# The first mixer's order without memory units, and the memory's products in the later mixer

## The chip, the cores and the metric

The kernel runs on one NeuronCore of a Trainium2 chip. The metric is the device time of one execution in microseconds; all times here are microseconds unless marked ns. Of the core's engines, TensorE (PE) does matrix products and transposes, with its weight loads (PEld) overlapping; VectorE (DVE) and ScalarE (ACT) do elementwise work and evictions; GpSimd (POOL) does little; SyncE (SP) issues nearly all transfers. Each engine runs its instructions in the order in which they were put on it, and waits at the first whose inputs or buffers are not ready.

## The reference

Two blocks in a row over one sequence of 256 tokens of width 1024, all in fp32. The first has two layers; a layer is a mixer, a residual with layer norm, a feed-forward (a dense SwiGLU in layer 0, eight experts with the top two per token in layer 1), and another residual with layer norm:

```
proj = x @ w_in        # columns for three branches
o_a  = gated delta rule (6 heads, 4 chunks of 64 tokens; S_c+1 depends on S_c), normed, times silu(gate)
u    = glu_a * sigmoid(glu_b);  u = causal depthwise conv of 31 taps + bias;  o_b = silu(layer_norm(u))
o_c  = softmax attention (6 heads, causal, decayed by a cumulative log-sigmoid)
mix  = (concat(o_a, o_b, o_c) * mix_scale) @ w_out
```

The second block has two layers too. Its mixer computes, besides a local attention, an attention over a memory: `k, v = split(rms_norm(mem) @ w_mem_kv)`, with four heads of 128 columns for k and 512 columns for v. The memory is an input, so k and v of both layers can be computed at any time before they are used.

## The kernel before

All weights are streamed once from HBM, in the order in which they are used, by transfers on SP's queue into four buffers called `raw`. A product is done in one of two ways. A split product first takes the weights apart, `hi` on ACT (L202) and `lo` on DVE (L206), and then does three matmuls in a reduced fp32 form (`mm3`: high with high, high with low, low with high). A whole product takes `raw` as it is, in one fp32 matmul instruction that the profile lists as two records; in the first mixer these read `x,raw`, and in a memory unit `raw` alone. The matmul line is L217 for all of them, so one goes by the names of tiles.

The first mixer (`_mixer1`, for l = 0 and 1) begins with the split projections for q, k and v of the gated delta rule. Then it prepares that rule's chunks: powers of a triangular matrix for its inverse (`XT`, `A`, `X`, `zc`), decays (`dec`), and the transformed keys and values. Then come the chunk steps: `ps_sm<-vn,kd` (c0, and then c1 and c2), each followed on DVE by `S<-S,eg,ps_sm`, then on PE by `S,wT` and on DVE by `vn<-u,ps_sm`. In between, work that doesn't depend on it is put in by a table: `fill(p)` (called from `gdn` and once behind it with `REST`) reads a string letter by letter. A letter c takes the next piece of the remaining projections, each of them 4 whole or 8 split products: first for the attention's values, then the rest of the delta rule's v, the attention's q and k in three groups, the convolution's two inputs (`gb`, `ga`, from which DVE makes `uu`), and the gate. An x takes the next step of the attention's six heads: scores and mask on PE, `fmx` on DVE, exponential `fp` on ACT, a reciprocal and a scaling on DVE, three transposes on PE, and for each pair of heads the product with the values (`fpT,fv`). A digit n takes n steps of the convolution: first `cvacc<-uu,cdwh,pc`, then 30 taps, each of two DVE instructions. U loads the memory (`mem_load`, with a scaling on ACT), and u does one memory unit (`mem_units`): a quarter of the memory's k and v of one layer, 16 whole products of 256 columns, evicted on ACT (`kvt`) and sent from ACT's queue to a buffer `kv` in HBM. The table `UNITS` says which units are done where: b3 to b5 lie in the blocks behind, m0 and m1 in the first mixer of layers 0 and 1.

After `REST` come the statistics of the convolution (`ps_st<-cst,cvacc`), its layer norm, the gated output of the delta rule (`og`), and the product with `w_out`.

Which instruction stands where on an engine is set when the program is built: a scheduler takes, for each engine, ready work in the order of the program, from a model of durations. So a change in the table moves the instructions of all engines near it.

In the second block's mixer, `mem_kv` makes k and v of the memory: for the units that were done it loads `kv` (L1652) and scales it into `km` and `vm`; for those that were not, it loads the memory (L1660), splits it (`mmh` on ACT, `mml` on DVE) and does split products.

Of the kernel before, what the change touches and what calls it, by code (L numbers as in the profile page):

```python
# [160 lines left out]
FREE = 1  # L161
PRE = 2
FILL = ({'s': 'cccc', 'g': 'cccccc'}, {'s': 'cccc', 'g': 'cccccc'})
REST = 'ccccxccxcxcxcxcxcxcxcccx33x33U333c3c3c3cu999u'
WHOLE = ('wwwpppwwpw', 'pwwpppwwpw')
PG = 2
MO = 6
# [1 line left out]
XRG = 6  # L169
SPLIT = 4  # L170
SPARE = ('xgh', 'xgl')
UNITS = {'b1': (), 'b2': (), 'b3': ((0, 0), (0, 1)), 'b4': ((0, 2),), 'b5': ((0, 3),), 'm0': ((1, 0), (1, 1)), 'm1': ((1, 2), (1, 3))}
SETUP = (2, 5)

SHIFT = 8
# [5 lines left out]
class K:  # L181
# [478 lines left out]
    def ffn_block1(self, l):  # L660
        with self.phase() as self.ph:
            z, st, ev = self.resid_ln()
            self.ffn('s1', 'ffn_w1', 'ffn_w3', 'ffn_w2', l, ev, mid=self.mem_stats,
                     mid2=(lambda: self.mem_load('b2')) if UNITS['b2'] else None)
            b = self.ln_finish(st, D, 1e-5)
# [61 lines left out]
    def _mixer1(self, l, first):  # L727
# [90 lines left out]

        units = list(UNITS[f"m{l}"])
        box = {}  # L820

        def fill(p):
            for n in p:
                if n == 'c':
                    next(stream, None)
                elif n == 'x':
                    next(box['fox'], None)
                elif n == 'U':
                    self.mem_load(f"m{l}")
                elif n == 'u':  # L830
                    if units:
                        self.mem_units(f"m{l}", [units.pop(0)])
                else:
                    for _ in range(int(n)):
                        next(conv, None)
# [34 lines left out]
        oS = self.gdn(l, qkv, lr, g, lnb, fill)  # L870
        fill(REST)
        mh, ml = self.new_hl()
# [727 lines left out]
    def mem_load(self, *at):  # L1600

        self.mts = {}
        for l in sorted(set(l for a in at for l, _ in UNITS[a])):
            mt = self.raw().rearrange("p (k t) -> p k t", k=KD)
# [5 lines left out]
    def mem_units(self, at, us=None):  # L1610


        for l, u in us or UNITS[at]:
            mt = self.mts[l]
# [372 lines left out]
```

## Time and profile before

| what | us |
|---|---|
| median of three runs | 2951.46 (2949.2 to 2954.4) |
| profiled execution | 2954.75, its span 2952.9 |
| PE busy | 2894.1 (98%), 19525 instructions |
| PE's weight loads busy | 2628.7 (89%) |
| DVE busy | 2155.8 (73%) |
| ACT busy | 1754.5 (59%) |
| mean granted clock of PE | 0.983 |

Busy is the time in which an engine has work; matmuls overlap, so that their listed durations add to more than the time from one start to the next. What an instruction costs in a dense stretch is read from the starts of its neighbours. The granted clock is the share of full speed (2.4 GHz) that the chip allowed PE; 0.50 is its lower level, 1.2 GHz.

### The profile page before, as it was taken

What the parts mean: (1) busy time and instruction counts of PE and PEld (TensorE: products, weight loads), DVE (VectorE), ACT (ScalarE), POOL (GpSimd) and SP (SyncE); (2) the same over time, 40 slices, a digit from 0 to 9 for tenths busy, and PEclk for the clock granted to TensorE, in tenths of its full rate; (3) what the DMA queues carried; (4) which work ended last, traced back from release to release, by engine and by line L of the source; (5) the groups of instructions that cost most, each with busy time, mean ns of one, the idle gap of its engine ahead of it and who ended that gap; (6) DMA issues with size and microseconds to landing.
All of it is one profiled execution on the core that took longest, in us unless ns stands there. A gap on an engine that the chain in (4) does not pass through costs nothing.

```text
span 2952.9 us, 48784 instructions
## 1 busy us (share of the span) xinstructions
PE 2894.1 (98%) x19525; PEld 2628.7 (89%) x19525; DVE 2155.8 (73%) x3156; ACT 1754.5 (59%) x2582; POOL 79.8 (3%) x142
## 2 busy tenths in 40 slices
PE   8999999999999999999999999999999999999998
PEld 7889998887888887788878899989999999999998
DVE  6476566479989888988889866676766665867764
ACT  5335445258787777778777744565554444655543
POOL 1100002000000000000000000100000000100000
PEclk9899999899999999999999999999999999999999
DMA  6035542158989997998999755534655555335553
GB/s 226 22 136 186 188 151 99 38 225 350 345 339 358 362 359 296 361 353 331 357 368 357 275 175 188 177 108 158 211 188 192 184 191 193 137 110 194 203 189 112
DMA packets 104205, 663.77 MB, mean 225 GB/s; under 512 B 11808, under 2 KB 17952, under 8 KB 28576
## 3 DMA queue, kind: packets, MB, share of 16 engines
q1 hardware_dynamic: 101664, 658.46, 60.6%
q8 instruction: 156, 2.56, 0.3%
q10 hardware_dynamic: 2304, 2.10, 0.2%
q14 instruction: 81, 0.66, 0.1%
HBM read 657.36 MB, written 3.15 MB: 224 GB/s over the span
## 4 chain that ended last, share of the span: by engine, by line
PE 57%; DVE 2%; ACT 1%; issue 0%; POOL 0%; POOLq 0%; DVEq 0%; ACTq 0%
PE ps_mm L217 47%; PE py L217 5%; PE ps_fx L217 2%; PE ps_sm L217 2%; DVE lo L206 1%; PE ps_fx L227 0%; PE ps_sm L227 0%; DVE aa L1784 0%; ACT hi L202 0%; DVE gi L206 0%; PE ps_st L217 0%; DVE aa L206 0%; ACT xr L203 0%; DVE y L214 0%; DVE ffab L206 0%
## 5 line engine op out<-in xcount | busy, mean ns | idle before, releaser
L206 DVE TENSOR_TENSOR lo<-raw,hi 128x1024 fp32r<-128x1024 f32 (+2 forms) x1216 | 1434.3, 1207 | 384.2 <-ACT hi L202 371.8
L202 ACT ACTIVATE hi<-raw 128x1024 fp32r<-128x1024 f32 (+2 forms) x1216 | 1246.8, 1044 | 622.0 <-PE ps_mm L217 466.7
L217 PE MATMUL ps_mm<-xh,hi 128*128 128x256 f32 x2736 | 777.1, 285 | 13.1 <-ACT hi L202 8.1
L217 PE MATMUL ps_mm<-xh,lo 128*128 128x256 f32 x2736 | 770.2, 282 | 2.1 <-DVE lo L206 2.1
L217 PE MATMUL ps_mm<-xl,hi 128*128 128x256 f32 x2736 | 771.8, 282 | 0.3 <-DVE xl L206 0.3
L217 PEld LDWEIGHTS ps_mm<-xh,hi 128*128 128x128 f32 x2736 | 519.5, 190 | 19.7 <-ACT hi L202 8.8
L217 PEld LDWEIGHTS ps_mm<-xh,lo 128*128 128x128 f32 x2736 | 518.6, 190 | 5.7 <-issue 2.7
L217 PEld LDWEIGHTS ps_mm<-xl,hi 128*128 128x128 f32 x2736 | 520.5, 190 | 3.5 <-issue 2.0
L217 PE MATMUL ps_mm<-lo,xgh 128*128 128x512 f32 x896 | 356.5, 398 | 0.7
L217 PE MATMUL ps_mm<-hi,xgl 128*128 128x512 f32 x896 | 349.8, 391 | 0.0
L217 PE MATMUL ps_mm<-hi,xgh 128*128 128x512 f32 x896 | 349.6, 392 | 0.0
L217 PE MATMUL ps_mm<-ffl,hi 128*128 128x256 f32 x880 | 245.6, 279 | 0.0
L217 PE MATMUL ps_mm<-ffh,hi 128*128 128x256 f32 x880 | 245.6, 279 | 0.0
L217 PE MATMUL ps_mm<-ffh,lo 128*128 128x256 f32 x880 | 245.5, 279 | 0.0
L217 PEld LDWEIGHTS ps_mm<-lo,xgh 128*128 128x128 f32 x896 | 168.4, 188 | 48.4 <-DVE lo L206 16.3
L217 PEld LDWEIGHTS ps_mm<-hi,xgh 128*128 128x128 f32 x896 | 168.5, 188 | 35.6 <-ACT hi L202 0.2
L217 PEld LDWEIGHTS ps_mm<-hi,xgl 128*128 128x128 f32 x896 | 168.6, 188 | 32.5
L217 PE MATMUL py<-lo,hh 128*128 128x512 f32 x448 | 178.5, 398 | 0.5
L217 PE MATMUL py<-hi,hl 128*128 128x512 f32 x448 | 174.8, 392 | 0.5
L217 PEld LDWEIGHTS ps_mm<-ffl,hi 128*128 128x128 f32 x880 | 165.4, 188 | 0.0
L217 PEld LDWEIGHTS ps_mm<-ffh,lo 128*128 128x128 f32 x880 | 165.4, 188 | 0.0
L217 PEld LDWEIGHTS ps_mm<-ffh,hi 128*128 128x128 f32 x880 | 165.4, 188 | 0.0
(433 smaller groups left out, 3735.7 us busy)
## 6 DMA issues: line engine op xcount, KB each, us to landing
raw<-in_sm SPq DMA_DIRECT2D x336, 1024.0 KB, 6.9
raw<-in_s SPq DMA_DIRECT2D x248, 1024.0 KB, 4.8
raw<-in_s SPq DMA_DIRECT2D x40, 512.0 KB, 3.3
raw<-in_s SPq DMA_DIRECT2D x32, 256.0 KB, 2.9
raw<-in_mem SPq DMA_DIRECT2D x5, 1024.0 KB, 4.9
kv<-kvt ACTq DMA_DIRECT2D x16, 128.0 KB, 5.4
raw<-kv SPq DMA_DIRECT2D x16, 128.0 KB, 2.8
raw<-in_s SPq DMA_DIRECT2D x2, 1005.0 KB, 6.7
```

What stands on the lines that cost most here:

```text
L202: return self.nc.scalar.activation(out, in_, func, scale=scale, **kw)
L206: return self.nc.vector.tensor_tensor(out=out, in0=a, in1=b, op=op)
L217: return self.nc.tensor.matmul(out, lhsT=l, rhs=r, start=start, stop=stop, skip_group_check=True, **kw)
```

## The change

Two tables change. `REST` loses its U and its two u, and is put in another order: the projections (c) come first, the attention's steps (x) alternate with three taps each (3), and there is one piece of projection less ahead of them. `UNITS` is empty for m0 and m1; so the four units of the second block's layer 1, which were done there, are not done ahead, and `mem_kv` makes that layer's k and v with split products. Units b3 to b5, which are those of layer 0, stay.

```diff
@@ -161,7 +161,7 @@
 FREE = 1
 PRE = 2
 FILL = ({'s': 'cccc', 'g': 'cccccc'}, {'s': 'cccc', 'g': 'cccccc'})
-REST = 'ccccxccxcxcxcxcxcxcxcccx33x33U333c3c3c3cu999u'
+REST = 'ccccccxcccccccc3x3x3x3x3x3x3x3x3xcccc39'
 WHOLE = ('wwwpppwwpw', 'pwwpppwwpw')
@@ -169,7 +169,7 @@
 XRG = 6
 SPLIT = 4
 SPARE = ('xgh', 'xgl')
-UNITS = {'b1': (), 'b2': (), 'b3': ((0, 0), (0, 1)), 'b4': ((0, 2),), 'b5': ((0, 3),), 'm0': ((1, 0), (1, 1)), 'm1': ((1, 2), (1, 3))}
+UNITS = {'b1': (), 'b2': (), 'b3': ((0, 0), (0, 1)), 'b4': ((0, 2),), 'b5': ((0, 3),), 'm0': (), 'm1': ()}
 SETUP = (2, 5)
```

In number of instructions as the program issues them: PE loses 64 whole products of units and gets 96 split matmuls of 256 columns and 48 of 512. DVE gets 8 `lo` and 8 `mml` more. ACT gets 8 `hi` and 8 `mmh` more and loses 8 evictions `kvt`, 8 transfers of them and 16 scalings of the memory. SP loses two loads of the memory in the first mixers and 8 of `kv`, and gets one of the memory in the later mixer. Everything else is the same in number.

On PE, in the first mixer of layer 0, around the first chunk step, this stood before. Here `fp` transposes belong to the attention's third head, and `x,raw` are pieces of the projections; `cr,selt` and what follows are the scores of a head.

```order
L217 MATMUL ps_sm<-XT,kbe 64x128 x6
L217 MATMUL ps_sm<-vb,XT 128x64 x6
L227 MATMUL ps_fx<-cst,fp 128x128
L217 MATMUL ps_sm<-vn,kd 128x128 x3
L227 MATMUL ps_fx<-cst,fp 128x128 x2
L217 MATMUL ps_mm<-x,raw 128x256
L217 MATMUL ps_sm<-S,wT 64x128 x3
L217 MATMUL ps_mm<-x,raw 128x256
L217 MATMUL ps_mm<-cr,selt 128x256
L217 MATMUL ps_mm<-selt,cr 128x256
L217 LDWEIGHTS identb
```

And this is the same place now.

```order
L217 MATMUL ps_sm<-XT,kbe 64x128 x6
L217 MATMUL ps_sm<-vb,XT 128x64 x6
L217 MATMUL ps_mm<-x,raw 128x256
L217 MATMUL ps_sm<-vn,kd 128x128 x3
L217 MATMUL ps_mm<-x,raw 128x256
L217 MATMUL ps_mm<-cr,selt 128x256
L217 MATMUL ps_mm<-selt,cr 128x256
L217 MATMUL ps_sm<-S,wT 64x128 x3
L217 LDWEIGHTS identb
L217 MATMUL ps_mm<-mkb,identb 128x128
L217 MATMUL ps_mm<-fb 128x128
```

The transposes of heads are gone from the place, since the first head now comes behind c0. In layer 0, 31 `x,raw` stand between the last split projection and c0 (before, 14) and no head's scores (before, three); in layer 1 it is 32 (before, 17) and none (before, four).

On DVE, in the same stretch, this stood before, from the first `vn` to the third.

```order
L206 TENSOR_TENSOR vn<-u,ps_sm 64x384
L214 SCALAR_TENSOR_TENSOR S<-S,eg,ps_sm 64x64 x6
L694 TENSOR_REDUCE fmx<-ps_mm 128x1 x2
L206 TENSOR_TENSOR vn<-u,ps_sm 64x384
L705 RECIPROCAL fsum<-fsum 128x2
L210 TENSOR_SCALAR fp<-fp,fsum 128x128
L210 TENSOR_SCALAR fp<-fp,fsum 128x256
L214 SCALAR_TENSOR_TENSOR S<-S,eg,ps_sm 64x64 x6
L206 TENSOR_TENSOR vn<-u,ps_sm 64x384
```

Now `uu` stands around the first `vn`, and the convolution's first taps (`cvacc`) between the chunk steps.

```order
L214 SCALAR_TENSOR_TENSOR uu<-fb,ps_mm 128x256
L206 TENSOR_TENSOR vn<-u,ps_sm 64x384
L214 SCALAR_TENSOR_TENSOR uu<-fb,ps_mm 128x256
L211 TENSOR_SCALAR cvacc<-uu,cdwh_368,pc 128x256 x2
L214 SCALAR_TENSOR_TENSOR cvacc<-uu,cdwh_368,cvacc 128x255
L214 SCALAR_TENSOR_TENSOR S<-S,eg,ps_sm 64x64 x6
L214 SCALAR_TENSOR_TENSOR cvacc<-uu,cdwh_368,cvacc 128x255
L214 SCALAR_TENSOR_TENSOR cvacc<-uu,cdwh_368,cvacc 128x254
L206 TENSOR_TENSOR vn<-u,ps_sm 64x384
L214 SCALAR_TENSOR_TENSOR cvacc<-uu,cdwh_368,cvacc 128x254
L694 TENSOR_REDUCE fmx<-ps_mm 128x1 x2
L214 SCALAR_TENSOR_TENSOR S<-S,eg,ps_sm 64x64 x6
```

Behind this piece the remaining five heads follow one another with two to eight taps between a head's steps, and the last ten taps without one. Before, `uu` came behind the third `vn` and the third head of this stretch, and of the 60 tap instructions 48 stood in one run.

On PE at the end of the stretch, `ps_mm<-raw x32` stood directly ahead of `ps_st<-cst,cvacc`; now three matmuls of the output projection stand there, and ahead of them the last value products and the last seven `x,raw` of the gate.

On PE in the second block's mixer of layer 1, ahead of the memory's attention (`km,cq`), there stood before split projections `xh,hi` and so on of the gate among the transposes of the local attention's heads.

```order
L217 MATMUL ps_mm<-xh,lo 128x256
L217 MATMUL ps_mm<-xh,hi 128x256
L217 MATMUL ps_mm<-xl,hi 128x256
L217 MATMUL ps_sm<-km,cq 128x256 x4
L217 MATMUL ps_mm<-xh,lo 128x256
```

Now the place ends with the products of the memory's values, 48 of 512 columns without a break, behind 96 of 256 columns for the keys.

```order
L217 MATMUL ps_mm<-hi,mmh 128x512
L217 MATMUL ps_mm<-lo,mmh 128x512
L217 MATMUL ps_mm<-hi,mml 128x512
L217 MATMUL ps_sm<-km,cq 128x256 x4
L217 MATMUL ps_mm<-xh,hi 128x256
```

The gate's projections that stood ahead of `km,cq` before now stand behind it, as filler of the memory's attention. On DVE the `mml` and `lo` of the memory stand one by one among the `fmx`, `ss` and `fp` of the local attention, and four `lo` of the value weights in one run ahead of the memory attention's first `fmx`.

## Rows read from the trace of the kernel before

**Rows 1.** The page's first part: busy time, share of the span and instructions of each engine.
```profile
PE 2894.1 (98%) x19525; PEld 2628.7 (89%) x19525; DVE 2155.8 (73%) x3156; ACT 1754.5 (59%) x2582; POOL 79.8 (3%) x142
```

**Rows 2.** Windows of the span: the stretch, its length, then for PE, PEld, DVE, ACT and POOL the busy time with the number of instructions, PE's granted clock, the share of the DMA engines and the rate. The first and the fourth are the preparation of the chunks in layers 0 and 1, the second and the fifth the chunk steps with all to the end of the taps, the third lies in the dense feed-forward of layer 0, and the last is the second block's mixer of layer 1 from its attention to the memory's attention.
```profile
87.00:132.00 45.00, 44.65 (x292) 38.44 (x292) 14.94 (x35) 16.37 (x51) 3.29 (x2) 0.81 0.00 1
132.50:183.50 51.00, 51.00 (x308) 42.05 (x308) 33.65 (x98) 15.47 (x39) 0.00 (x0) 1.00 0.27 88
300.00:350.00 50.00, 50.00 (x431) 50.00 (x430) 28.88 (x36) 24.39 (x37) 0.00 (x0) 1.00 0.54 186
505.00:552.00 47.00, 47.00 (x273) 41.27 (x272) 11.70 (x28) 15.16 (x47) 3.28 (x2) 0.67 0.06 23
552.70:601.00 48.30, 48.30 (x292) 39.69 (x291) 32.42 (x93) 14.37 (x38) 0.00 (x0) 1.00 0.21 72
2575.00:2631.00 56.00, 52.81 (x355) 44.30 (x354) 42.98 (x129) 36.36 (x102) 0.00 (x0) 0.94 0.27 95
```

**Rows 3.** Timeline of PE, in layer 0 and then in layer 1: start, length, engine, line, operation, output and inputs, shape and number of records, and in brackets an idle time ahead with what ended it.
```profile
132.48 0.93 PE L217 MATMUL ps_sm<-vn,kd 64*128 64x128 f32 x6
...
169.77 13.98 PE L217 MATMUL ps_mm<-raw 128*128 128x256 f32 x64
183.58 0.95 PE L217 MATMUL ps_st<-cst,cvacc 128*128 128x1 f32 x8
...
552.65 0.93 PE L217 MATMUL ps_sm<-vn,kd 64*128 64x128 f32 x6
...
587.15 13.98 PE L217 MATMUL ps_mm<-raw 128*128 128x256 f32 x64
600.97 0.95 PE L217 MATMUL ps_st<-cst,cvacc 128*128 128x1 f32 x8
```

**Rows 4.** Timeline of DVE in layer 0, from the first `vn` on, with the same columns.
```profile
135.16 0.56 DVE L206 TENSOR_TENSOR vn<-u,ps_sm 64x384 f32<-64x384 f32 x1 [6.27 <-PE ps_sm L217]
136.94 1.38 DVE L214 SCALAR_TENSOR_TENSOR S<-S,eg,ps_sm 64x64 f32<-64x64 f32 x6 [1.23 <-PE ps_sm L217]
...
143.33 1.37 DVE L214 SCALAR_TENSOR_TENSOR S<-S,eg,ps_sm 64x64 f32<-64x64 f32 x6
...
156.81 0.75 DVE L214 SCALAR_TENSOR_TENSOR uu<-fb,ps_mm 128x256 f32<-128x256 f32 x2 [1.56 <-PE ps_mm L217]
157.47 0.73 DVE L211 TENSOR_SCALAR cvacc<-uu,cdwh,pc 128x256 f32<-128x256 f32 x2
...
161.45 0.62 DVE L694 TENSOR_REDUCE fmx<-ps_mm 128x1 f32<-128x128 f32 x2
...
163.15 0.16 DVE L705 RECIPROCAL fsum<-fsum 128x2 f32<-128x2 f32 x1
...
163.60 0.54 DVE L210 TENSOR_SCALAR fp<-fp,fsum 128x128 f32<-128x128 f32 x2
164.06 18.17 DVE L214 SCALAR_TENSOR_TENSOR cvacc<-uu,cdwh,cvacc 128x249 f32<-128x249 f32 x48
182.16 1.08 DVE L206 TENSOR_TENSOR xl<-fo,xh 128x256 fp32r<-128x256 f32 x3
```

**Rows 5.** The window of the taps in layer 0, first with all instructions, then with those on `cvacc` alone (here without POOL's column).
```profile
157.50:182.20 24.70, 24.70 (x141) 21.65 (x141) 24.61 (x69) 6.61 (x16) 0.00 (x0) 1.00 0.42 137
...
157.50:182.20 24.70, 0.00 (x0) 0.00 (x0) 23.69 (x62) 0.00 (x0) 1.00 0.42 137
```

**Rows 6.** Timeline of PE: two matmuls of 512 columns, the first and the seventh of a dense stretch in the experts, and a whole memory unit of 32 records.
```profile
702.48 0.40 PE L217 MATMUL py<-hi,hh 128*128 128x512 f32 x1
...
703.86 0.39 PE L217 MATMUL py<-hi,hh 128*128 128x512 f32 x1
...
1676.74 7.07 PE L217 MATMUL ps_sm<-raw 128*128 128x256 f32 x32
```

**Rows 7.** The second block's mixer of layer 1: a row of DVE's timeline, one of PE's, and a window behind them.
```profile
2575.69 3.49 DVE L206 TENSOR_TENSOR lo<-raw,hi 128x1024 fp32r<-128x1024 f32 x3
...
2579.70 1.26 PE L217 MATMUL ps_sm<-k,qs 64*128 64x128 f32 x4 [3.06 <-DVE ss L214]
...
2580.00:2585.00 5.00, 5.00 (x18) 3.48 (x17) 5.00 (x19) 2.34 (x10) 0.00 (x0) 0.51 0.38 129
```

**Rows 8.** Timeline of PE in layer 0: from the start of a head's scores to what follows them, a value product, and products `x,raw` at a lower and at the full clock.
```profile
88.42 0.47 PE L217 MATMUL ps_mm<-cr,selt 128*128 128x256 f32 x1
...
90.54 0.88 PE L227 MATMUL ps_sm<-cst,XT 128*128 128x128 f32 x6
...
103.90 0.87 PE L217 MATMUL ps_fx<-fpT,fv 128*64 128x128 f32 x6
...
112.95 1.20 PE L217 MATMUL ps_mm<-x,raw 128*128 128x256 f32 x2
...
152.72 2.86 PE L217 MATMUL ps_mm<-x,raw 128*128 128x256 f32 x12
```

**Rows 9.** Windows of 5 in the preparation of the chunks, with the columns of rows 2.
```profile
105.00:110.00 5.00, 5.00 (x23) 4.05 (x23) 1.37 (x2) 0.97 (x2) 0.00 (x0) 0.55 0.00 0
110.00:115.00 5.00, 5.00 (x24) 4.78 (x22) 0.00 (x0) 0.82 (x2) 0.00 (x0) 0.50 0.00 0
510.00:515.00 5.00, 5.00 (x24) 4.45 (x23) 0.00 (x0) 1.24 (x4) 1.64 (x1) 0.50 0.00 0
```

**Rows 10.** Evictions of the units over the span, by length (shortest, median, longest, in ns) and first and last start.
```profile
L202 ACT ACTIVATE kvt<-ps_mm x14: 359/384/386, 176.9 to 1675.2; 128x256 f32<-128x256 f32 x14
```

## The prediction

> **What bounds the kernel now.** I read the page's busy line first: PE holds work for 98% of the span, DVE for 73% [rows 1]. Such an average hides which engine ends a stage, so I next cut the two passes of the first mixer into stretches [rows 2]. From 132.5 to 183.5 (layer 0) and 552.7 to 601 (layer 1) PE is busy without a gap, at the full clock. Before them, from 87 to 132 and 505 to 552, PE is also busy, but at a mean clock of 0.81 and 0.67, and DVE has little to do (14.94 and 11.70).
>
> Then I read the timeline of PE for the end of each stretch. It closes with 64 records `ps_mm<-raw`, the 32 whole products of two memory units: 169.77 to 183.58, so 13.8, and 587.15 to 600.97, the same [rows 3]. Right behind stands `ps_st<-cst,cvacc`, the convolution's statistics, from which the chain to the mixer's output goes on. That looks as if the units ended the stage. But the timeline of DVE shows the taps running from 157.47 to 182.16 without a pause [rows 4], and the windows give DVE 24.61 busy of 24.70, 23.69 of it on `cvacc` [rows 5]. So two things end together: DVE's taps at 182.2, PE's units at 183.58. The units cost PE 13.8 a layer, and in that time DVE would have kept `ps_st` waiting anyway until 182.2. Only both moved together gain, and the change moves both: units out, and `uu` earlier.
>
> Of the Trainium skill's "Perfetto Trace Analysis", section "Identifying the Most-Contended Engine", one rule bears here: matmul busy share is no measure of how near TensorE is to its peak, while for the vector engine occupancy is a fair one. The trace agrees: at the same PE 100% the weight loads take 42.05 of 51.00 in the tail of layer 0 and 50.00 of 50.00 in a dense stretch [rows 2]. By it DVE is the truer bound of the tail; by matmul busy share alone it would be PE, and the sum that of the first rival below.
>
> **The change, part by part.** Four pieces of work move.
>
> *(a) Added in the later mixer, layer 1.* The K and V products of the memory come back as split products: 96 matmuls of 256 columns and 48 of 512. In the window 300:350, 431 matmuls of 256 columns fill 50 us: 0.116 each [rows 2]; 96 make 11.1. Matmuls of 512 columns start at 702.48 and, six steps on, at 703.86: 0.23 each [rows 6]; 48 make 11.0. The window 2575:2631, in which they would fall, has PE busy 52.81 of 56.00 [rows 2], so they can hide in 3.2 at the most. Filler now spent between attention steps goes to them, so I take no hiding, and +0.8 for the new splits on ACT and DVE standing among the softmax steps: 22.9. Those splits are 8 `lo` of 1.2 and 8 `mml` of 256 columns, some 13 of DVE time in a window where DVE holds 42.98 of 56; the four kv loads and evictions that go are off the path. Bounds: 19 (all of PE's idle time filled) to 27 (a stall like the 3.06 at 2579.70, when PE waited for `ss` behind three `lo` on DVE, and half clock for 5 us behind it [rows 7]).
>
> *(b) The start of the chunk chain, c0 (`ps_sm<-vn,kd`).* In front of it the order now has 31 x,raw products in place of 14 in layer 0 and 32 in place of 17 in layer 1, and no attention heads instead of three and four. A product costs 0.45 at full clock (six in 2.86 from 152.72, less 0.17 by which the last record overlaps, as the 64 records of a unit pair are listed with 13.98 and end after 13.81) and 1.0 at half (1.20 at 112.95, less 0.2); a head's scores cost 2.12 (88.42 to 90.54), the value product of a pair 0.8 (0.87 at 103.90, less overlap) [rows 3, 8]. Layer 0: 17 x 0.45 = 7.6 against 3 x 2.12, some 0.8 of transposes and two value products of 0.8 = 8.8, so -1.2 at full clock. But the stretch runs at 0.55 and 0.50 from 105 to 115 [rows 9], and there what was light becomes x,raw at 1.0. Bounds -1.2 to +3; I take +0.7. Layer 1: 15 x 0.45 = 6.8 against 4 x 2.12 + 1.1 + 2 x 0.8 = 11.2, so -4.4 at full clock; there the value products ran at half clock (0.50 from 510 to 515 [rows 9]), which gives back more, and so did some scores. I take -4.8, bounds -6 and -1.
>
> *(c) The tail, c0 to the last tap.* Now DVE carries from c0: `uu` 0.66, the tap's first step 0.65, taps 22.95 (157.47 to 182.16 less init and one head's 1.1), three `vn` of 0.55 less overlap (1.5), two `S` of 1.39 (2.8), and six heads at 1.08 (0.62 `fmx`, 0.16 reciprocal and 0.54 `fp` by their rows, less some 0.08 of overlap each): 6.5 [rows 4]. Sum 35.1. At the start taps can't fill everything, since each `vn` and `S` waits for PE: before, c0 to `S` was 132.48 to 136.94 and the second `S` began at 143.33. In the new order 6 taps and one head stand in that time, which leaves 4.5 of waiting; the heads' exponentials on ACT (`fmx` at 161.45 to reciprocal at 163.15 is 1.7, and two or three taps of 0.38 fill most of it) leave some 1.9 more. Tail 41.5. PE's own work in it is 51.1 (c0 to 183.58 [rows 3]) less the units 13.8, less 17 products 7.6, plus the three heads 8.8: 38.5, so DVE is the bound, by 3. Bounds: 38.5 (DVE hides) and 45 (both wait in turn, which a fixed order on both engines makes possible).
>
> Layer 0: 132.48 + 0.7 + 41.5 = 174.7 against 183.58: -8.9. Layer 1: 552.65 - 4.8 + 41.5 = 589.4 against 600.97: -11.6 [rows 3].
>
> *(d) What follows `ps_st`.* ACT no longer evicts the units there; two evictions of a unit's halves stood at 184.4 and 185.2, among the statistics, at 0.38 each with a wait for the transfer behind them [rows 10]. So -0.8 to 0; I take -0.5 for each layer, since ACT's queue has a gap there too. The four `raw` buffers bound how far the weight stream can run ahead, and products that are done earlier free them earlier, so I cost SP's queue at nothing; if the next weights came late, ACT's `hi` for the output projection would show it.
>
> Sum: -8.9 - 0.5 - 11.6 - 0.5 + 22.9 = +1.4. On the profiled execution's 2954.75 that is 2956.1. Against the median of the three runs, 2951.46, which is 3.3 below the profiled execution, it is **2952.9**, no change that can be measured: 0.2%, about what a measurement of this kernel tells from no change, is 5.9.
>
> **The rivals.**
>
> *1. PE is what counts everywhere, and DVE hides.* Then the change is worth its PE time: four units, 27.6 (twice 13.8; one alone is listed with 7.07 at 1676.74 [rows 6]), against +22.1: -5.5, and with 2 more from (b) and (d) some -7.5: 2944. For it: PE 100% in both tails. Against it: DVE 99.6% in the last 24.7, and six heads more beside the taps. By the Trainium skill's "FP8 and Floating Point Precision", section "TensorE Precision Notes", a true fp32 product takes four passes of the array, so that a split one in three saves a quarter; here a whole product takes 0.44 and a split one 3 x 0.116 = 0.35, which agrees nearly (0.79). By the rule the four units' 27.6 would come back as 20.7 and not 22.1, and the sum would be 0.0.
>
> *2. The units were free and the tail does not shorten: slower.* If the new order makes DVE and PE wait for each other (heads need PE scores, ACT exponentials, DVE sums, and all stand in a fixed order between taps and chunk steps), the tail is longer than 46; it then gains only 4.4 in layer 0 and 7.1 in layer 1, and with PE idle the clock can fall as it did behind 2579.70 (0.51 from 2580 to 2585 [rows 7]). With (a) at 22.9 to 27 the sum is +11 to +15: 2964. It decides from a tail of about 44 up. For it: PE's fill work is spent before c0, so nothing covers the chain there. Against it: three more heads are there as cover.
>
> *3. The clock of the chunk preparation stays up.* From 105 to 115 and 510 to 515 PE's work is small matmuls at half clock [rows 9]. The new order puts other products between them, and if the granted clock then stays at 1.0, at most (1 - 0.81) x 45 = 8 in layer 0 and (1 - 0.67) x 47 = 15 in layer 1 come back [rows 2]. With half of it the sum is -10: 2941. Against it: products stand between the small ones already, and the clock falls nevertheless.
>
> **How the numbers follow.** The forecast (within 5 of +1.4) 0.50, rival 1 0.20, rival 2 0.20, rival 3 0.10. Range: 2942 to 2964, which takes in rival 1, half of rival 3 and rival 2's near end; the forecast's own range is 2947 to 2958. Faster by over 0.2%, that is below 2945.6: 0.10 from rival 3, 0.13 from rival 1 and a little from the forecast's lower side, 0.27. Slower, above 2957.4: 0.20 from rival 2 and 0.08 from the forecast's upper side, 0.28. The rest, 0.45, is the same.
>
> **What would show it.** (a) In the later mixer's second layer 96 and 48 new matmuls, and the stretch to the last `fpT,vm` longer by 20 to 25. (b) `vn,kd` of layer 0 near 133 and of layer 1 near 538 (4.8 earlier by (b), 9.4 by layer 0). (c) `uu` on DVE within 3 us of c0, the last tap 39 to 44 behind c0, and PE with gaps of 2 to 5 before `ps_st`. (d) `ps_st` to the first `xl<-G` within 1 of what it was. Wrong would be: a tail over 45 or under 38, PE idle over 6 in the later mixer, or a granted clock above 0.9 in the chunk preparation.

## The result and the profile after

The changed kernel took 2981.11 (median of four runs, 2979.52 to 2995.43) against 2952.93 for the kernel before beside it: a ratio of 1.011, interval 1.0081 to 1.0138. The forecast was 2952.9 with 2942 to 2964; the time lies 28 above the forecast and 17 above the range. A second set of four runs of the same kernel had a median of 2984.91 (2974.19, 2975.43, 2994.4 and 2996.1) and a ratio of 1.0109 (1.0064 to 1.0153). The profiled execution took 2979.52, its span is 2977.7, 24.8 more than before.

The busy line of the page answers to [rows 1]: PE gained 10, and is still at 98%.

```profile
PE 2904.3 (98%) x19541; PEld 2631.2 (88%) x19541; DVE 2169.7 (73%) x3172; ACT 1756.0 (59%) x2574; POOL 77.5 (3%) x142
```

The stage that was forecast to shrink did not. These are windows of the profile after, with the columns of [rows 2]: in layer 0 the preparation of the chunks (from the first `A<-dec` on POOL to c0, the first `vn,kd`) and the tail (c0 to `ps_st`), and the same two in layer 1.

```profile
71.50:139.10 67.60, 66.53 (x378) 57.15 (x376) 27.65 (x61) 18.86 (x49) 14.57 (x12) 0.77 0.13 47
139.10:192.80 53.70, 48.74 (x262) 35.77 (x262) 36.23 (x111) 15.72 (x49) 0.00 (x0) 0.81 0.06 20
497.00:552.10 55.10, 52.74 (x364) 44.17 (x362) 29.01 (x61) 20.79 (x57) 14.12 (x12) 0.97 0.17 58
552.10:604.70 52.60, 47.93 (x262) 34.43 (x261) 36.47 (x111) 15.84 (x49) 0.00 (x0) 0.84 0.06 21
```

The tails last 53.8 and 52.5, where before they lasted 51.1 and 48.3 [rows 3] and 41.5 was forecast. Neither engine is full in them: DVE is busy for 36.2 of 53.7, and PE for 48.7, at a granted clock of 0.81. The two preparations moved in opposite ways: the first is longer than before (62.3, from 70.22 to 132.48) at a clock of 0.77, the second shorter (69.6, from 483.10 to 552.65) at 0.97.

The timeline of PE in layer 0 shows where the tail breaks. It answers to the first three of [rows 3].

```profile
139.07 0.93 PE L217 MATMUL ps_sm<-vn,kd 64*128 64x128 f32 x6
...
157.60 0.50 PE L227 MATMUL ps_fx<-cst,fp 128*128 128x128 f32 x3
159.94 0.38 PE L217 MATMUL ps_mm<-cr,selt 128*128 128x256 f32 x1 [1.84 <-ACT fp L203]
...
167.03 0.58 PE L217 MATMUL ps_mm<-cr,selt 128*128 128x256 f32 x1 [1.37 <-ACT fp L203]
...
172.90 0.58 PE L217 MATMUL ps_mm<-xh,hi 128*128 128x256 f32 x1 [1.38 <-ACT fp L203]
...
192.83 0.95 PE L217 MATMUL ps_st<-cst,cvacc 128*128 128x1 f32 x8
```

Three times PE stands before the next scores, or before a piece of the gate, until ACT has done a head's exponential `fp`. Scores and pieces of projection write `ps_mm`, of which there are three buffers, and the exponential, which reads a head's scores, is what empties one. After the first of these waits the granted clock falls: the columns of [rows 9] read 1.00 from 155 to 160 and 0.50 from 165 on.

```profile
155.00:160.00 5.00, 3.16 (x28) 2.28 (x26) 3.89 (x13) 2.08 (x7) 0.00 (x0) 1.00 0.00 0
165.00:170.00 5.00, 3.63 (x14) 2.56 (x12) 3.67 (x13) 1.28 (x5) 0.00 (x0) 0.50 0.00 0
175.00:180.00 5.00, 5.00 (x19) 3.34 (x19) 3.91 (x12) 0.78 (x2) 0.00 (x0) 0.50 0.01 2
```

On DVE, whose rows answer to [rows 4], `uu` comes 1.6 behind c0, as forecast. But then the heads' reciprocals wait for the exponentials, up to 5.31 at 184.22. The first of PE's three waits begins here: counted in order, the second head's scores stood on PE from 145.61 to 148.7, but its maximum `fmx` comes on DVE at 157.05 only, behind a chunk step's `S` and `vn`, which waited for PE (0.89 and 1.91), and six taps.

```profile
140.67 0.42 DVE L214 SCALAR_TENSOR_TENSOR uu<-fb,ps_mm 128x256 f32<-128x256 f32 x1 [7.16 <-PE ps_mm L217]
...
154.98 2.04 DVE L214 SCALAR_TENSOR_TENSOR cvacc<-uu,cdwh,cvacc 128x253 f32<-128x253 f32 x5
157.05 0.62 DVE L694 TENSOR_REDUCE fmx<-ps_mm 128x1 f32<-128x128 f32 x2
157.59 1.25 DVE L214 SCALAR_TENSOR_TENSOR cvacc<-uu,cdwh,cvacc 128x250 f32<-128x250 f32 x3
159.91 0.17 DVE L705 RECIPROCAL fsum<-fsum 128x2 f32<-128x2 f32 x1 [1.07 <-ACT fp L203]
...
167.01 0.17 DVE L705 RECIPROCAL fsum<-fsum 128x2 f32<-128x2 f32 x1 [1.32 <-ACT fp L203]
...
172.88 0.17 DVE L705 RECIPROCAL fsum<-fsum 128x2 f32<-128x2 f32 x1 [2.44 <-ACT fp L203]
...
176.80 0.61 DVE L694 TENSOR_REDUCE fmx<-ps_mm 128x1 f32<-128x128 f32 x2
...
184.22 0.17 DVE L705 RECIPROCAL fsum<-fsum 128x2 f32<-128x2 f32 x1 [5.31 <-ACT fp L203]
...
188.50 3.75 DVE L214 SCALAR_TENSOR_TENSOR cvacc<-uu,cdwh,cvacc 128x230 f32<-128x230 f32 x10
```

Why the exponential ahead of 184.22 is late is read from ACT's timeline. ACT takes its work in the order in which it stands: the copy of the earlier head's transposes (`fpT`), the eviction of its value product (`fo`), which waited 2.70 for PE, the split `hi` for the gate, which waited 2.14 for PE, and only then the exponential at 183.29, whose maximum DVE had begun at 176.80.

```profile
176.53 0.49 ACT L202 ACTIVATE fpT<-ps_fx 128x384 f32<-128x384 f32 x1 [3.68 <-PE ps_fx L227]
179.71 0.47 ACT L202 ACTIVATE fo<-ps_fx,pc 128x256 f32<-128x256 f32 x1 [2.70 <-PE ps_fx L217]
182.33 1.06 ACT L202 ACTIVATE hi<-raw 128x1024 fp32r<-128x1024 f32 x1 [2.14 <-PE ps_mm L217]
183.29 0.35 ACT L203 ACTIVATE fp<-ps_mm,fmx 128x128 f32<-128x128 f32 x1
```

So three engines in fixed order wait for each other in turn: PE for ACT's exponential, ACT for PE's products at half clock, DVE for ACT. The sums of DVE's waits from 139.5 to 193 are these (who waited, for whom, total, times, longest); of the 7.2 for `uu`, which began before c0, 1.6 lies behind it.

```profile
DVE fsum L705 <- ACT fp L203: 10.5, 5, 5.3
DVE uu L214 <- PE ps_mm L217: 7.2, 1, 7.2
DVE vn L206 <- PE ps_sm L217: 4.3, 3, 1.9
DVE S L214 <- PE ps_sm L217: 0.9, 1, 0.9
```

The later mixer went as forecast. A norm's `rms_r` on POOL stands ahead of the stretch with the second block's last mixer, and one behind it. Before, these were at 2505.21 and 2758.42 (the first two rows here), now at 2506.91 and 2783.32: 276.41 against 253.21, +23.2.

```profile
2505.21 0.70 POOL L525 TENSOR_TENSOR rms_r<-rms_v,cst 128x2 f32<-128x2 f32 x1 [185.39 <-DVE rms_v L211]
...
2758.42 0.70 POOL L525 TENSOR_TENSOR rms_r<-rms_v,cst 128x2 f32<-128x2 f32 x1 [194.93 <-DVE rms_v L211]
...
2506.91 0.70 POOL L525 TENSOR_TENSOR rms_r<-rms_v,cst 128x2 f32<-128x2 f32 x1 [185.40 <-DVE rms_v L211]
...
2783.32 0.70 POOL L525 TENSOR_TENSOR rms_r<-rms_v,cst 128x2 f32<-128x2 f32 x1 [218.14 <-DVE rms_v L211]
```

By the starts of such milestones (the first `A<-dec` of each layer, c0, `ps_st`, the norms' rows on POOL), the 24.8 come together so:

| stretch | us against before |
|---|---|
| up to the first `A<-dec` | +1.3 |
| preparation, layer 0 | +5.3 |
| tail, layer 0 | +2.7 |
| from `ps_st` to the preparation of layer 1 | +4.7 |
| preparation, layer 1 | -14.4 |
| tail, layer 1 | +4.2 |
| from there to the second block's last mixer | -2.0 |
| that mixer | +23.2 |
| behind it, and rounding | -0.2 |

### The profile page after: what moved, and what is told of

The parts are those of the page before. It is cut to its first block, busy times and chain, and to the rows that moved or that the text cites. A ratio compares the mean times of both kernels' runs of the same rounds, so it can differ in the third digit from the quotient of the medians.

```text
span 2977.7 us, 48812 instructions
## 1 busy us (share of the span) xinstructions
PE 2904.3 (98%) x19541; PEld 2631.2 (88%) x19541; DVE 2169.7 (73%) x3172; ACT 1756.0 (59%) x2574; POOL 77.5 (3%) x142
## 4 chain that ended last, share of the span: by engine, by line
PE 58%; DVE 2%; ACT 1%; issue 0%; POOL 0%; POOLq 0%; DVEq 0%; ACTq 0%
PE ps_mm L217 47%; PE py L217 5%; PE ps_fx L217 2%; PE ps_sm L217 2%; DVE lo L206 1%; PE ps_sm L227 0%; PE ps_fx L227 0%; DVE aa L1784 0%; ACT hi L202 0%; DVE gi L206 0%; PE ps_st L217 0%; DVE aa L206 0%; ACT xr L203 0%; DVE y L214 0%; DVE ffab L206 0%
```

## The experiments

Theory A said that the new order makes PE wait for the exponentials and that half clock follows; the tails would shrink where the heads have work between them, or where the taps no longer stand in their way. The rivals were that the units were worth their PE time (B), that the units' absence alone makes the tail slow (C), that DVE's own work lasts 53 (D), that the heads' chain is as slow without taps (G), and, for the preparations, that the clock differs between executions (E) or is fixed by the order (F). The tails and preparations of all kernels stand in a table behind.

**Only the units out.**

```diff
-REST = 'ccccxccxcxcxcxcxcxcxcccx33x33U333c3c3c3cu999u'
+REST = 'ccccxccxcxcxcxcxcxcxcccx33x33333c3c3c3c999'
-... 'm0': ((1, 0), (1, 1)), 'm1': ((1, 2), (1, 3))}
+... 'm0': (), 'm1': ()}
```

> Only the units are taken out (UNITS empty for m0 and m1, REST as before without U and u); the order of all else stays. Theory A (the new order of heads and taps makes PE wait for the heads' exponentials, and half clock follows): without the new order there are no such waits; DVE's taps still end where they did, so each tail (first vn,kd to ps_st) is shorter by 1.4 at most (49.7 in layer 0, 46.9 in layer 1), and the later mixer costs +23: 2971 to 2975. Rival B (the units were PE time on the path): each tail loses 13.8, total 2944 to 2950. Rival C (units out is what makes the tail slow, for want of filler): tails of 52 to 54 as in the changed kernel, total about 2980.

It took 2988.52 (ratio 1.0124, 1.0104 to 1.0145), more than the whole change. The tails are 46.7 and 45.6, so 13.8 of PE's work gave back 4.4 and 2.7. PE's waits from 130 to 190 show why: after the last projection it stands for the taps.

```profile
PE ps_st L217 <- DVE cvacc L214: 11.2, 1, 11.2
```

That is theory A's reading of the kernel before, a little more generous (4.4 and 2.7 where 1.4 at most was said), and refutes B and C: the units were nearly free where they stood. The time is 14 above the 2971 to 2975 expected. In its profile 9.3 of that is the first preparation, 71.6 at a clock of 0.79 (62.3 before), of which more below. Another part lies right behind the tails: from `ps_st` to the following residual norm it took 39.8 and 44.6, where before it took 36.9 and 39.2. So what the missing units gave back in the tails, 7.1, was lost again behind them, 8.2. Behind PE's wait the granted clock is 0.50 from 185 to 195; that the clock alone costs these 8.2 is not shown.

```profile
190.00:195.00 5.00, 5.00 (x25) 5.00 (x25) 2.74 (x6) 0.00 (x0) 0.15 (x1) 0.50 0.00 0
```

**Only the order.**

```diff
-REST = 'ccccxccxcxcxcxcxcxcxcccx33x33U333c3c3c3cu999u'
+REST = 'ccccccxcccccccc3x3x3x3x3x3x3x3x3xUcccc3u9u'
```

> Only the order: REST as changed, but the units kept, loaded behind the last head and done around the last taps; the later mixer as before. Theory A: the same three waits for fp of 1.4 to 1.8 and the same half clock behind them as in the changed kernel, tails of 53 to 66 (52.5 to 53.8 plus what of the units' 13.8 does not fit beside the last taps), total 2955 to 2975. Rival C: the units fill, tails of 51 to 54, PE without waits, total 2945 to 2955.

It took 2967.17 (1.0076, 1.0046 to 1.0107). The three waits are there: PE for `fp` 4.1 in three pieces from 120 to 195. The tails are 68.2 and 63.7, above the expected 66 in layer 0, at a clock of 0.85 and 0.89: the units stand behind the heads, too late to fill their waits, and the tails are 14.4 and 11.2 longer than the changed kernel's, about the units' 13.8. So the order does the harm, with the units or without. Its two preparations ran at full clock, 52.2 and 52.4 long.

```profile
70.00:122.20 52.20, 51.16 (x370) 42.92 (x369) 25.66 (x59) 17.35 (x48) 14.57 (x12) 1.00 0.09 31
122.20:190.30 68.10, 63.96 (x331) 49.14 (x331) 39.50 (x115) 18.75 (x53) 0.00 (x0) 0.85 0.17 61
```

**The gate's pieces between the heads** (the changed kernel otherwise).

```diff
-REST = 'ccccccxcccccccc3x3x3x3x3x3x3x3x3xcccc39'
+REST = 'ccccccxcccccccc3x3xc3x3xc3x3xc3x3xc3x39'
```

> The changed kernel with one thing moved: the last four pieces of projection (the gate's) stand between the heads and not behind them. Theory A: they fill the waits for fp, the granted clock of the tail stays above 0.9, the tails fall to 42 to 47, total 2960 to 2968. Rival D (DVE's own work, taps and six heads, is what lasts 53): tails stay at 52 to 54, total 2978 to 2983.

It took 2966.91 (1.0044, 1.0026 to 1.0063). The tails fell to 47.5 in both layers, just past the upper end of theory A's 42 to 47, with the clock at 0.93 and 0.94. DVE did the same work, 35.5 against 36.2, so rival D is out. In layer 0 DVE's waits for the exponentials fell from 10.5 to 5.4, and PE's from 4.6 in three pieces to 2.3 in two. The time is within the 2960 to 2968 expected.

```profile
138.10:185.60 47.50, 43.96 (x262) 32.05 (x261) 35.53 (x110) 15.15 (x46) 0.00 (x0) 0.93 0.13 45
```

**The taps behind the heads** (the changed kernel otherwise).

```diff
-REST = 'ccccccxcccccccc3x3x3x3x3x3x3x3x3xcccc39'
+REST = 'ccccccxccccccccxxxxxxxxxcccc39999'
```

> The changed kernel with the taps taken from between the heads: all nine steps of the heads first, then the gate's pieces, then the taps. Theory A, in the form that DVE's fixed order (taps ahead of fmx and of the scaling) holds the exponentials and through them PE: no wait of PE for fp above 1 and no half clock among the heads, the heads done 22 to 28 behind c0, the taps behind them on DVE alone, tails of 41 to 47. Rival G (the heads' chain through PE, ACT and PSUM is as slow without the taps): the same waits of 1.4 and the half clock, tails of 52 and more.

It took 2972.78 (1.0043, 1.0013 to 1.0073). No wait for `fp` is left on PE in the tail of layer 0, and the clock is 1.00 from 136 to 176; instead PE stands for the last taps, and behind that the clock is 0.50 again, from 181 to 191.

```profile
PE ps_st L217 <- DVE cvacc L214: 7.0, 1, 7.0
```

The tails are 48.1 and 47.7, 0.7 to 1.1 above theory A's range, far below rival G's 52. The heads were not done within 28 of c0, as expected, but at 34.7. So DVE's fixed order, taps ahead of the heads' maxima, does hold the exponentials, and with it gone 5.7 and 4.8 of the tails go; that is about half of what they lay above the 41.5 forecast. Part of it is lost again behind them: from `ps_st` to the residual norm it took 39.6 and 43.9, in the changed kernel 37.7 and 41.0.

**Both repairs.**

```diff
-REST = 'ccccccxcccccccc3x3x3x3x3x3x3x3x3xcccc39'
+REST = 'ccccccxccccccccxxxcxxcxxcxxc39999'
```

> The changed kernel with both repairs: the taps taken from between the heads, and the gate's four pieces spread between them. Theory A: DVE's wait for the exponentials falls to 3 or less (10 in the changed kernel), PE's waits for fp vanish, and the tails come to the 41.5 that DVE's work asks for, 41 to 45; the total stays above the kernel before, by the later mixer's +23 less 5 to 9 a layer: 2955 to 2975, by the clock of the preparations. Rival G (with either repair the rest is the chunk chain's own waits): tails of 46 to 48, as with each repair alone.

It took 2972.02 (1.0075, 1.004 to 1.0111), and here theory A's number failed: the tails are 48.0 and 47.8, as with either repair alone, which is what rival G said of this kernel. DVE no longer waits for the exponentials, but for the scores instead, 6.5 in six pieces from 125 to 172, since the pieces of the gate now stand ahead of them on PE.

```profile
DVE fmx L694 <- PE ps_mm L217: 6.5, 6, 2.9
DVE vn L206 <- PE ps_sm L217: 3.6, 3, 1.5
```

So 47.5 is what these orders reach; the 41.5 of the forecast was reached by none, since DVE's work of 35.5, the chunk chain's waits of 5.8 and these 6.5 already make 47.8 here.

**The units among the heads**, all four, with the gate's pieces between the last heads.

```diff
-REST = 'ccccxccxcxcxcxcxcxcxcccx33x33U333c3c3c3cu999u'
+REST = 'ccccccxccccccccU3x3xu3x3x3xu3x3xc3xc3xcc39'
```

> The changed order with the four units kept, one behind the first head's step and one in the middle, and the gate's pieces between the last heads; the later mixer as before. Theory A: PE has work in all waits, so the tails are PE's 38.5 plus 13.8, 52 to 54, at a granted clock above 0.95; the total then depends on the start of the chunk steps (+5 and -14 against before, as in the changed kernel): 2940 to 2955. Rival D (DVE lasts 53 by itself and units on PE delay the heads more): tails of 58 and more, total above 2960.

It took 2962.05 (1.002, 0.9999 to 1.0042), which is not told from the kernel before, but is 7 above theory A's range and within rival D's times. PE is full at full clock in both tails, 56.9 and 54.3 long: about PE's own work, as theory A said, though they are 2.9 and 0.3 above its range; rival D's 58 was not reached.

```profile
135.90:192.80 56.90, 56.82 (x339) 44.58 (x339) 41.07 (x116) 21.48 (x57) 0.00 (x0) 1.00 0.26 93
552.00:606.30 54.30, 54.30 (x333) 42.81 (x332) 40.11 (x116) 23.11 (x64) 0.00 (x0) 1.00 0.27 98
```

**Half of the units**, the keys' two, one in each first mixer.

```diff
-REST = 'ccccxccxcxcxcxcxcxcxcccx33x33U333c3c3c3cu999u'
+REST = 'ccccccxccccccccU3x3xu3x3xc3x3xc3x3xc3x3xc39'
-... 'm0': ((1, 0), (1, 1)), 'm1': ((1, 2), (1, 3))}
+... 'm0': ((1, 0),), 'm1': ((1, 1),)}
```

> Two units kept, one in each first mixer between the heads, and the gate's pieces spread between the later heads; so the later mixer computes only the memory's values by split products, 48 matmuls of 512 columns. Theory A: tails of PE's 38.5 plus 6.9, 45 to 49, at a clock above 0.95, and the later mixer longer by 11 to 12: total 2940 to 2955, depending on the clock of the preparations. Rival D (DVE and the heads' chain last by themselves): tails of 51 and more, total above 2958.

It took 2959.94 (1.002, 0.9998 to 1.0043), at the median 5 above the expected range, within noise of the kernel before; it is also above the 2958 of rival D. The tails are 50.7 and 48.5, the first 1.7 above theory A's range and both under rival D's 51, with PE at full clock and busy for all but 0.5, so it is PE that lasts. The later mixer is 11.8 longer by the same rows of POOL, within the 11 to 12 that half of the products was to cost. Each unit in a filled tail costs PE about what it gives back in the later mixer, so nothing is won by moving them.

**The two kernels once more, unchanged**, for the clock of the preparations.

> The changed kernel once more, unchanged, for its clock in the preparation of the chunks. Theory E (whether PE is granted the full clock there is not fixed by the kernel but differs between executions): the two preparations (first A<-dec to first vn,kd) differ from the first profile's 67.6 and 55.1 by 5 or more in one layer at least, and the times spread by 10 or more; the two tails stay at 52 to 54. Rival F (fixed by the order of the instructions): 67.6 and 55.1 again within 2, and times within 4.

> The kernel before once more, unchanged, for the same. Theory E: one of the preparations, 62.3 and 69.5 in the first profile, differs by 5 or more; the tails stay at 51.1 and 48.3 within 0.5. Rival F: all four again within 2. Time 2946 to 2964 by either.

The changed kernel (2984.91) had tails of 52.7 and 51.6 again, the second 0.4 under the range. But its first preparation lasted 54.0 at full clock and its second 64.9 at 0.79, the other way round than in the first profile.

```profile
70.00:124.00 54.00, 52.94 (x378) 44.43 (x377) 27.70 (x61) 18.42 (x49) 14.61 (x12) 1.00 0.17 59
...
480.00:544.90 64.90, 63.71 (x365) 54.57 (x363) 28.01 (x61) 21.15 (x57) 14.65 (x12) 0.79 0.14 49
```

The same instructions in the same order differ by 13.6 and 9.8 between two executions. In layer 0 PE was idle for 1.1 in both, so it is the granted clock that differs: theory E for the changed kernel, and F is out. Its eight times lie near 2975, 2980 and 2995, steps as large as such differences; in the second four alone the mean granted clock is 0.981 and 0.98 in the two runs near 2975, 0.973 and 0.972 in the two near 2995. The kernel before (2954.18, ratio 1.0011, 0.999 to 1.0033) had its tails to the hundredth, 51.10 and 48.32, and preparations of 65.1 and 68.2 at a clock of 0.82 in both. They differ from the first profile's by 2.8 and 1.4, less than theory E asked for and, in layer 0, more than F.

All profiles side by side, from the starts on the timelines, with the granted clock of the preparations in brackets; the last mixer's difference is the one between the same two `rms_r` as above.

| kernel | prep. 0 | tail 0 | prep. 1 | tail 1 | last mixer | span |
|---|---|---|---|---|---|---|
| before | 62.3 (0.86) | 51.1 | 69.6 (0.78) | 48.3 | 0 | 2952.9 |
| before, again | 65.1 (0.82) | 51.1 | 68.2 (0.82) | 48.3 | +1.7 | 2958.0 |
| changed | 67.6 (0.77) | 53.8 | 55.1 (0.97) | 52.5 | +23.2 | 2977.7 |
| changed, again | 54.0 (1.00) | 52.7 | 64.9 (0.79) | 51.6 | +23.3 | 2972.4 |
| units out | 71.6 (0.79) | 46.7 | 67.0 (0.82) | 45.6 | +22.1 | 2987.3 |
| order | 52.2 (1.00) | 68.2 | 52.4 (1.00) | 63.7 | +1.1 | 2965.3 |
| gate between | 66.0 (0.79) | 47.5 | 52.6 (1.00) | 47.5 | +23.3 | 2965.4 |
| taps behind | 66.0 (0.79) | 48.1 | 61.7 (0.83) | 47.7 | +23.6 | 2977.7 |
| both | 53.9 (1.00) | 48.0 | 66.5 (0.77) | 47.8 | +22.1 | 2970.7 |
| units among | 64.4 (0.76) | 56.9 | 56.1 (0.88) | 54.3 | 0 | 2960.7 |
| half the units | 65.2 (0.76) | 50.7 | 56.7 (0.88) | 48.5 | +11.8 | 2964.2 |

## Why the prediction was wrong

*(a), the later mixer: right.* 22.9 was forecast, +23.2 and +23.3 came, and +11.8 with half of the products. The 48 matmuls of 512 columns ran from 2623.73 to 2634.93, 11.2 where 11.0 was worked out, and the wait for `ss` was the same 3.1 as before.

*(c), the tail: wrong, and this is the step that failed.* The term that broke is the "some 1.9 more" for the heads' exponentials; in layer 0 they cost 10.5. The other two terms were nearer: DVE's work came to 36.2 for 35.1, the chunk chain's waits to 6.8 (with 1.6 for `uu` behind c0) for 4.5. So 8.6 of the miss of 12.3 is the exponentials'; in layer 1 they cost 9.7. I took the time from `fmx` to the reciprocal, 1.7 in the row before, as ACT's own, with taps to cover it. But in that row ACT had stood idle for 5.73 until DVE had this head's maximum:

```profile
162.16 0.37 ACT L203 ACTIVATE fp<-ps_mm,fmx 128x128 f32<-128x128 f32 x1 [5.73 <-DVE fmx L694]
```

In the new order ACT's earlier entries wait for PE, and PE waits for ACT to empty a buffer. The term was too small for the repaired orders too: with the gate between the heads DVE's waits for exponentials come to 5.4 in layer 0, with the taps behind to 5.7 for exponentials and scores together, with both to 6.5 for scores alone. With 53.8 and 52.5 for 41.5 the miss is 12.3 and 11.0, together 23.3; put into the sum in place of 41.5 it gives 2956.1 + 23.3 = 2979.4, against 2979.52 for the profiled execution. So near a fit is partly luck: (b) gave 5.0 less than forecast, and what lies between the stages some 5 more.

*That DVE bounded the tail before, and that the units were nearly free there: right, shown.* With only the units out, PE stood 11.2 for the taps, the tails shrank by 4.4 and 2.7 of 13.8, and what follows them grew by 2.9 and 5.3. That DVE would bound the new tail was wrong: it is busy for 36.2 of 53.7 there.

*(b), the start of the chunk steps: wrong, in both directions, and not a fault of the order alone.* Forecast +0.7 and -4.8 for c0, the preparations moved by +5.3 and -14.4 in the first profile and by -8.3 and -4.7 in the second, counted against the first profile of the kernel before. What the order asks for at full clock is near 54 in layer 0 (54.0 at 1.00) and 53 in layer 1 (52.6 at 1.00, with the gate between the heads); the rest is the granted clock, which the order does not fix. That -4.7 meets the -4.8 of the forecast is luck, since it came at a clock of 0.79. Rival 3 hoped that the clock stays up, and in one layer of each profile it did, one of the signs named of being wrong; its prices of at most 8 and 15 are close to the -8.3 and -14.4 of these two.

*(d): wrong in sign, small.* From `ps_st` to the following residual norm it took 0.8 and 1.7 more, not 0.5 less.

*The rivals.* Rival 2 was the one that happened: heads, taps and chunk steps wait for each other in fixed order, and PE's waits are followed by half clock. Its condition, a tail above 46, held, but its price, +11 to +15, was worked out from a tail at the condition's edge and not from the chain itself. The bound of 45 for the tail was a guess with no row under it. Rival 1 is refuted by the run with only the units out. The Trainium skill's "Perfetto Trace Analysis", section "Identifying the Most-Contended Engine", holds matmul busy share for a poor measure of how near TensorE is to its peak. Here it was no measure of what the work was worth either: PE was at 100% in the tail of the kernel before, and with the units out it stood for 11.2. The Trainium skill's "Perfetto Trace Analysis", section "Optimization Strategy", says that the same gap, repeated on the engine that should be full, can mean too little SBUF or PSUM for the next tile. The three waits of 1.84, 1.37 and 1.38 for a buffer of `ps_mm` may be of that kind; a fourth buffer was not tried, so no run here shows it.

What stays open: what separates an execution in which the preparation runs at full clock from one in which it does not. That the changed order's is granted full clock more often than the old one's is suggested by six of sixteen preparations with the new front at 0.97 or above and none of six with the old one (the two kernels' first profiles, their second ones, and the experiments'), but the runs were not made to test it. Open too is why the half clock sets in: it reads 0.50 behind PE's waits in the tails, but in the preparations also where PE is busy without a gap ([rows 9]).

## What to carry to other kernels

When a stage is bounded by a chain over three engines, the sum of the busiest engine's work is only a lower bound of it; walk the queue of each engine behind each wait in the new order, and ask what stands ahead of the instruction that frees a buffer. Filler between the links of such a chain is worth more than filler behind it: the same four pieces of projection, placed between the heads and not behind them, took 4 to 6 off the tails, counted against the two profiles of the changed kernel. And where light matmuls run at a clock that differs between executions, take two profiles before a difference in that stretch is put down to a change.

## What was not expected of the hardware

The granted clock in the preparation of the chunks is not fixed by the program: with the same order on PE it was 0.77 and 1.00 in layer 0 and 0.97 and 0.79 in layer 1 in two executions, 13.6 and 9.8 apart. After the first of three waits of 1.4 to 1.8 in the tail, PE went on at the lower level, 1.2 GHz, for some 20 (0.61 from 160 to 165, 0.50 from 165 to 180), although it had been at the full clock for 30 before (1.00 from 130 to 160). Where PE stood for the last taps instead, 11.2 with only the units out and 7.0 with the taps behind the heads, the clock was 0.50 for some 10 behind the wait.
